# Single-transfer attention operands and new planner figures in a hybrid RWKV/attention layer

## The chip, the cores and the metric

The kernel runs on one core of a Trainium2 chip. The metric is device time in microseconds (us) of one execution; lower is better. Before the change the median of three runs is 1868.69 us (1868.56 to 1870.11).

## The reference

One decoder layer over 2048 positions of width 1024, all in float32. The input is normalised and modulated, and one projection makes the inputs of two groups of eight heads: an RWKV-7 recurrence, and a causal attention ("FoX") whose logits carry a running sum of log forget gates. Both results are gated, projected once more and normalised. Cut to what the change touches:

```python
proj = h @ w_in
q_f, k_f, v_f = (proj[..., a:b].reshape(B, T, 8, 64) for a, b in ...)
log_f = log_sigmoid(proj[..., FX_F0:FX_END] + fox_bf)
cum = cumsum(log_f, axis=1)
s = einsum('bhqd,bhkd->bhqk', q, k) * 64 ** -0.5 + cum[t] - cum[s]     # causal
y_b = softmax(s) @ v
```

## The kernel before, in words

The sequence is worked in two halves of 1024 positions, each in blocks of 512 columns. Each half has an RWKV stage and then an attention stage; the projection of w_in (66 weight tiles of 128 columns, each 48 matmuls over the two blocks of a half, 24 for a block) runs beside both and fills TensorE where the stages leave it free. A weight tile comes through a single staging buffer, `wst`, and is split by ScalarE and GpSimd into one of two buffers `wsp` (`weights`, the second generator after `plan`). All transfers are issued by SyncE, one after another, in the order in which the program was written out.

That order is made by a planner. The work is written as Python generators, and `Driver` (from line 117 on) runs them by a model of the engines: `Driver.cost` gives the duration of an instruction, `Driver.on_pe` that of a matmul by its place in the array, `Driver.time` when operands and buffers are free. The stream that can go on earliest is advanced next, and what it issues stands next on its engine's queue. The model's figures are used for nothing else, but every engine's order follows from them. For a transfer the model adds bytes over 300 GB/s and 2000 ns to the landing.

An attention logit is one fp32 product made of rounded parts. `ev_fox` stores a rounded part ("hi") and the rest ("lo") of q and k to DRAM (`qscr`, `kscr`; one tile for two heads, 128 rows of 1024 columns for hi and as many for lo; 16 evacuations of each). `ev_f` computes the running sum, its parts go to `cscr` as 3 rows per head. `qscr1` holds three rows for the q side (0, 1, 1).

In `fox_ops` each half asks for the operands of head after head: `q1` and `k1` have 67 rows (64 rows of hi and the three extra rows), `q2` and `k2` 128 rows (hi and lo). The tile pool has 21 such operands at a time. `conv` loads one operand with two transfers: 64 + 3 rows for `q1`, `k1`, and 64 + 64 rows for `q2`, `k2`. In `fox_guard` a first pass multiplies `q1` by `k1` to get the row maxima and writes their negative into one row of `q1` by a small transfer from `mrow`; `fox_s` then computes the logits from all four operands, `fox_pv` multiplies the exponentials by v. All instructions are recorded at line 134, the planner's `call`, so rows are read by tile names: `fx_s` are the attention operands, `fx_p` the exponentials, `ht` and `wsp` the projection's operands, `rw_s` the RWKV stage's, `ps` is PSUM, `arena` the general pool.

Of the kernel before, what the change touches and what calls it, by code (L numbers as in the profile page):

```python
# [9 lines left out]
F32 = mybir.dt.float32  # L10
# [8 lines left out]
TB = 1024  # L19
NB = 512  # L20
# [117 lines left out]
class Driver:  # L138
# [31 lines left out]
    def cost(self, e, op, ops, kw):  # L170
        out, ins = ops[0], ops[1:]
        n = max(a.free_size() for a in ops)
        sb = all(a.space != "PSUM" for a in ops)
        if "dma_start" in op:
            return 450.0 if e.name == "sp" else 1000.0
        if e.name == "act":
            return (94 if sb else 51) + 0.834 * n + 93 * sum(isinstance(kw.get(k), bass.AP) for k in ("scale", "bias"))
        if e.name == "dve":
            if op == "reciprocal":
                return 65 + 6.25 * n  # L180
            if op == "tensor_tensor_scan":
                return 69 + 2.15 * n
            if op == "tensor_tensor_reduce":
                return 180 + 1.04 * n
            ptr = 61 * sum(a.free_size() == 1 for a in ins[1:]) if "scalar" in op else 0
            if op in ("tensor_copy", "tensor_scalar", "memset") and sb:
                return 69 + 0.52 * n + ptr
            return 69 + 1.04 * n + ptr
        if op == "affine_select":
            return 137 + 0.834 * n  # L190
        if kw.get("op") == OP.pow:
            return 300 + 165 * n
        return 147 + 2.17 * n if op == "tensor_tensor" else 161 + 0.834 * n if op == "tensor_scalar" else 34 + 0.834 * n
# [17 lines left out]
    def on_pe(self, t, op, ops):  # L211

        m, n, k = ops[1].free_size(), ops[2].free_size(), list(ops[1].ap)[0][1]
        r0, c0 = ops[1].start_partition() // 32, ops[0].start_partition() // 32
        nr, nc = (1 if x <= 32 else 2 if x <= 64 else 4 for x in (k, m))
        one = ops[1].dtype == F32R or op == "transpose"
        stream, load = n * (1 if one else 2) / 2.4, m * 2 / 2.4
        if nr == nc == 4:
            d = max(stream + (14 if n >= 256 else 3), load + 2)
        else:  # L220
            d = max(stream + (load if nc < 4 else 6), 25.0)
        d *= 1 if one else 2
        t = max(t, self.pe.began + 7)
        if (nr, nc) != self.mode:
            t = max(t, max(max(x) for x in self.cells) + (100 if self.mode else 0))
            self.mode = (nr, nc)
        cells = [(i, j) for i in range(r0, min(4, r0 + nr)) for j in range(c0, min(4, c0 + nc))]
        t = max(t, max(self.cells[i][j] for i, j in cells))
        for i, j in cells:
            self.cells[i][j] = t + d  # L230
        self.pe.began = t + (0 if one else 7)
        self.pe.free = max(self.pe.free, t + d)
        return t + d
# [101 lines left out]
def hymba_kernel(ctx: ExitStack, tc, x, c, emb_ln_g, emb_ln_b, w_ada, b_ada, w_in, rwkv_mix, w0,  # L335
                 w_up, a0, a_up, k_k, k_a, r_k, gn_g, gn_b, fox_bf, w_out, ln_g, ln_b, out):
    nc = tc.nc
    drv = Driver()
    pe, act, dve, pool, sp = (Engine(drv, n, e) for n, e in (("pe", nc.tensor), ("act", nc.scalar),
                              ("dve", nc.vector), ("pool", nc.gpsimd), ("sp", nc.sync)))  # L340
# [3 lines left out]
    dram = ctx.enter_context(tc.tile_pool(name="dram", bufs=1, space=bass.MemoryType.DRAM))  # L344

    def dap(t, offset, ap):
        return bass.AP(tensor=t.tensor, offset=t.offset + offset, ap=ap)
# [34 lines left out]

    yscr = [dram.tile([D, TB], F32, name=f"yscr{i}") for i in range(2)]
    cscr = [dram.tile([3, 8, TB], F32, name=f"cscr{i}") for i in range(2)]
    fscr = [{k: [dram.tile([2, 128, TB] if k in "qk" else [128, TB], F32, name=f"{k}scr{h}{i}") for i in range(4)]
             for k in "qkvg"} for h in range(2)]
    qscr1 = dram.tile([3, 512], F32, name="qscr1")
    lowscr = [dram.tile([2, 128, 512], F32, name=f"lowscr{i}") for i in range(2)]
    lscr = dram.tile([128, 3, 512], F32, name="lscr")
    vscr = [[dram.tile([128, 512], F32, name=f"vscr{i}{h}") for h in range(2)] for i in range(4)]  # L390
# [185 lines left out]
    def start_consts():  # L576
# [52 lines left out]
        for i, pattern in enumerate(([[0, 32], [1, 4]], [[1, 2], [0, 64]], [[0, 2], [1, 64]])):  # L629
# [1 line left out]
            yield  # L631
            dve.tensor_copy(fb[:, i, :], jf)
            yield
        qr = yield from slots.get()
        pool.memset(qr.ap[0:3], 1.0)
        pool.memset(qr.ap[0:1], 0.0)
        sp.dma_start(qscr1, qr.ap[0:3])
# [180 lines left out]
    res = {}  # L818
# [147 lines left out]
    def ev_f(b, half, blk):  # L966

        z = yield from slots.get()
        z_ = z.ap[0:8]
        act.activation(z_, b.ap[0:8], AF.Identity, bias=bfc[0:8, 0:1])  # L970
        yield
        for i in range(1, 4):
            tt(z_, b.ap[32 * i:32 * i + 8], z_, OP.add)
            yield
        b.free()
        while nproj.get((half, blk), 0) < EF:
            yield 0
        e = yield from slots.get()
        u = yield from slots.get()
        w = yield from slots.get()  # L980
        e_, u_, w_ = e.ap[0:8], u.ap[0:8], w.ap[0:8]
        act.activation(e_, z_, AF.Abs)
        yield
        act.activation(e_, e_, AF.Exp, scale=-1.0)
        ts(z_, z_, 0.0, -8.0, OP.min, OP.mult)
        yield
        act.activation(u_, e_, AF.Ln, bias=1.0)
        ts(w_, e_, 1.0, None, OP.add)
        yield
        dve.scalar_tensor_tensor(z_, u_, 8.0, z_, op0=OP.mult, op1=OP.add)  # L990
        ts(w_, w_, -1.0, None, OP.add)
        yield
        act.activation(u_, u_, AF.Exp, scale=-1.0)
        tt(w_, e_, w_, OP.subtract)
        yield
        tt(w_, w_, u_, OP.mult)
        yield
        dve.scalar_tensor_tensor(z_, w_, 8.0, z_, op0=OP.mult, op1=OP.add)
        dve.memset(e_, 1.0)
        w.free()  # L1000
        while blk and ("f", half) not in flag:
            yield 0
        yield
        dve.tensor_tensor_scan(u_, e_, z_, bfc[0:8, 1:2], op0=OP.mult, op1=OP.add)
        yield
        dve.tensor_copy(bfc[0:8, 1:2], u_[:, 511:512])
        flag.add(("f", half))
        act.activation(z_.bitcast(F32R), u_, AF.Copy)
        yield
        tt(u_.bitcast(F32R), u_, z_, OP.subtract)  # L1010
        yield
        for i, t in enumerate((e_, z_, u_)):
            sp.dma_start(cscr[half][i, :, blk * NB:(blk + 1) * NB], t)
        for t in (z, e, u):
            t.free()

    def silu(b, g):

# [18 lines left out]
    def ev_fox(k):  # L1037
        def ev(b, half, p, blk):
            s = yield from slots.get(1)
            to = fscr[half][k][p]  # L1040
            cols = slice(blk * NB, (blk + 1) * NB)
            if k == "g":
                yield from silu(b, s)
            elif k == "v":
                act.activation(s.ap, b.ap, AF.Copy)
                b.free()
                yield
            else:
                l = yield from slots.get(1)
                act.activation(s.r, b.ap, AF.Copy)  # L1050
                yield
                tt(l.r, b.ap, s.ap, OP.subtract)
                b.free()
                i = int(k == "q")
                sp.dma_start(to[i, :, cols], s.ap)
                yield
                sp.dma_start(to[1 - i, :, cols], l.ap)
                l.free()
            if k in "vg":
                sp.dma_start(to[:, cols], s.ap)  # L1060
            s.free()
            yield
            res[half, p, k + "f", blk] = True
        return ev
# [575 lines left out]
    def fox_ops(half, st):  # L1640


        def conv(key, o, H, name, b4):
            while (b4 // 2, H // 2, name[0] + "f", b4 % 2) not in res:
                yield 0
            src = fscr[b4 // 2][name[0]][H // 2]
            c = (b4 % 2) * NB
            if name[1] == "2":
                for i in range(2):
                    sp.dma_start(o.f[hs(i)], src[i, hs(H % 2), c:c + NB])  # L1650
            else:
                sp.dma_start(o.f[0:64], src[int(name == "q1"), hs(H % 2), c:c + NB])
                sp.dma_start(o.f[64:67], cscr[b4 // 2][:, H, c:c + NB] if name == "k1" else qscr1)
            yield
            st["ops"][key] = o

        for H in range(8):
            for m in "12":
                for name, b0, b1 in (("q" + m, 2 * half, 2 * half + 2), ("k" + m, 0, 2 * half + 2)):
                    for b4 in range(b0, b1):  # L1660
                        o = yield from phase["slots"].get()
                        drv.spawn(conv((H, name, b4), o, H, name, b4), 1)
# [3 lines left out]
    def fox_guard(half, st):  # L1666
# [15 lines left out]
        def finish(H, qg, mx, left):  # L1682
# [17 lines left out]
            b.free()  # L1700
            mx.free()
            yield
            sp.dma_start(ops[H, "q1", qg].f[64:65].rearrange("o (j x) -> o j x", j=4), mrow[0:4, r].bitcast(F32))
            yield
            rowbuf.append(r)
            st["max"].add((H, qg))
# [398 lines left out]
```

## Time and profile before

| | before |
|---|---|
| median of 3 runs | 1868.69 us |
| the profiled execution's own time | 1866.47 us |
| its span, first to last instruction | 1864.7 us |
| mean granted TensorE clock | 0.98 of 2.4 GHz |
| transfers' packets | 172129, 181.60 MB |
| SyncE's queue: share of the 16 DMA engines' span | 30.6% |

The page gives each engine's busy time; a busy TensorE counts matmuls whose ends are modelled, so it isn't TensorE at its peak. Windows give the same for stretches of the span, with the granted clock (1.00 is 2.4 GHz, 0.50 is 1.2 GHz), the mean busy share of the 16 DMA engines and what they moved. The timeline names each instruction with start and duration, and in brackets the idle time before it and what ended that. The attention stages lie at about 600 to 880 us and 1300 to 1660 us, the RWKV stages before them; the tail after 1660 us is the output projection.

### The profile page before, as it was taken

The page shows a single profiled execution, that of the slowest core. Times are in us where ns is not written, and L with a number is a line of the kernel's source. Part 1 is how long each engine was busy: PE and PEld are TensorE (multiplying, and loading weights), DVE is VectorE, ACT ScalarE, POOL GpSimd, SP SyncE. Part 2 cuts the span into 40 slices and gives each one's busy share as a digit, 9 for nine tenths or more (in the row PEclk, how much of TensorE's full clock was granted, in tenths as well). Part 3 has the DMA queues.
Part 4 walks back from the last instruction along what each step waited for, and adds up shares of the span by engine and source line. Part 5 has one row for each costly group of instructions (what it writes and reads, how often), then busy time and mean ns, then how long its engine had stood idle before and what let it go on. Part 6 is the DMA issues. An engine that isn't in the chain of part 4 may idle for free.

```text
span 1864.7 us, 35565 instructions
## 1 busy us (share of the span) xinstructions
PE 1784.5 (96%) x13609; PEld 1288.3 (69%) x13609; DVE 1287.4 (69%) x3049; ACT 804.4 (43%) x1571; POOL 779.3 (42%) x773
## 2 busy tenths in 40 slices
PE   8999999999999899999999999989899899999995
PEld 6777777767777656677777777767555356666884
DVE  4987685665773768667657675762677584876998
ACT  2454555354444245554554554443244344432000
POOL 1333242422423357743143442424256364566652
PEclk8999999998999999999999999999899899999998
DMA  8252020210122755132021120213422732512433
GB/s 263 72 163 81 30 69 23 80 51 26 53 87 86 226 172 178 58 115 84 19 78 36 41 79 30 75 39 114 131 92 84 244 111 77 191 57 90 153 115 122
DMA packets 172129, 181.60 MB, mean 97 GB/s; under 512 B 12180, under 2 KB 116197, under 8 KB 171960
## 3 DMA queue, kind: packets, MB, share of 16 engines
q1 hardware_dynamic: 171960, 179.33, 30.6%
q8 instruction: 108, 1.77, 0.4%
q14 instruction: 61, 0.50, 0.1%
HBM read 132.10 MB, written 47.13 MB: 96 GB/s over the span
## 4 chain that ended last, share of the span: by engine, by line
PE 55%; DVE 5%; ACT 3%; SPq 3%; DMA 2%; issue 2%; POOL 1%; DVEq 0%; ACTq 0%; POOLq 0%
PE ps L134 55%; SPq L134 3%; ACT rw_s L134 2%; DVE rw_s L134 2%; DMA arena<-vscr 1%; DVE end_s L134 1%; DVE small L134 1%; DVE arena L134 1%; POOL rw_s L134 0%; POOL wsp L134 0%; DMA arena<-in_b_ada_dram 0%; ACT arena L134 0%; DMA yscr<-rw_s 0%; DVE fx_p L134 0%; DMA fx_s<-qscr 0%
## 5 line engine op out<-in xcount | busy, mean ns | idle before, releaser
L134 PE MATMUL ps<-ht,wsp 128*128 128x512 f32 x3840 | 976.4, 400 | 3.4 <-POOL wsp L134 1.3
L134 PEld LDWEIGHTS ps<-ht,wsp 128*128 128x128 f32 x3840 | 701.1, 189 | 163.3 <-issue 15.0
L134 POOL TENSOR_TENSOR wsp<-wst,wsp 128x1024 fp32r<-128x1024 f32 x79 | 192.8, 2440 | 320.2 <-ACT wsp L134 256.2
L134 ACT ACTIVATE rw_s<-ps 64x256 f32<-64x256 f32 (+3 forms) x544 | 215.9, 409 | 200.7 <-PE ps L134 101.0
L134 PE MATMUL ps<-fx_s 67*128 67x512 f32 (+6 forms) x960 | 261.1, 390 | 12.3 <-DMA fx_s<-kscr 4.0
L134 ACT ACTIVATE fx_p<-ps 128x512 f32<-128x512 f32 (+3 forms) x336 | 162.8, 521 | 196.2 <-PE ps L134 175.6
L134 PEld LDWEIGHTS ps<-fx_s 67*128 67x128 f32 (+1 forms) x960 | 165.4, 193 | 118.3 <-issue 47.7
L134 POOL TENSOR_TENSOR fx_p<-fx_p 128x512 f32<-128x512 f32 (+2 forms) x160 | 185.7, 1167 | 140.7 <-PE ps L134 138.3
L134 PE MATMUL ps<-rw_s 32*32 32x32 f32 (+4 forms) x5376 | 227.7, 217 | 17.0 <-DVE rw_s L134 8.0
L134 PEld LDWEIGHTS ps<-rw_s 32*32 32x32 f32 (+3 forms) x5376 | 195.7, 130 | 66.1 <-issue 26.6
L134 DVE TENSOR_TENSOR rw_s<-rw_s 128x24 f32<-128x24 f32 (+11 forms) x544 | 179.8, 336 | 26.0 <-ACT rw_s L134 12.6
L134 DVE TENSOR_REDUCE small<-ps 128x1 f32<-128x512 f32 (+1 forms) x208 | 134.5, 683 | 44.4 <-PE ps L134 43.6
L134 ACT ACTIVATE arena<-ps 128x512 f32<-128x512 f32 (+3 forms) x128 | 74.1, 581 | 191.6 <-PE ps L134 161.7
L134 POOL TENSOR_TENSOR small<-small,nhalf 128x8 f32<-128x8 f32 (+1 forms) x48 | 68.3, 1425 | 211.6 <-DVE small L134 211.5
L134 PE MATMUL ps<-fx_p,fx_v 128*64 128x512 f32 (+3 forms) x640 | 155.9, 556 | 0.0
L134 DVE TENSOR_TENSOR fx_p<-fx_p 128x512 f32<-128x512 f32 (+1 forms) x128 | 111.9, 874 | 51.6 <-POOL fx_p L134 48.9
L134 ACT ACTIVATE wsp<-wst 128x1024 fp32r<-128x1024 f32 x80 | 84.3, 1054 | 134.2 <-PE ps L134 110.1
L134 DVE TENSOR_SCALAR state<-ps,dl 64x64 f32<-64x64 f32 x256 | 72.4, 283 | 64.2 <-PE ps L134 57.2
L134 POOL TENSOR_TENSOR rw_s<-rw_s,arena 128x512 f32<-128x512 f32 x64 | 84.9, 1328 | 69.4 <-ACT arena L134 39.2
L134 DVE TENSOR_TENSOR arena<-ps,arena 128x512 fp32r<-128x512 f32 (+4 forms) x108 | 72.5, 677 | 54.0 <-ACT arena L134 50.3
L134 POOL TENSOR_SCALAR rw_s<-rw_s 64x128 f32<-64x128 f32 x128 | 38.0, 297 | 120.0 <-PE ps L134 109.4
L134 ACT ACTIVATE rw_s<-rw_s 32x256 f32<-32x256 f32 (+2 forms) x112 | 70.0, 653 | 39.4 <-DVE rw_s L134 38.7
(152 smaller groups left out, 1864.9 us busy)
## 6 DMA issues: line engine op xcount, KB each, us to landing
wst<-in_w_in_dram SPq DMA_DIRECT2D x66, 512.0 KB
fx_s<-kscr SPq DMA_DIRECT2D x144, 128.0 KB
fx_s<-qscr SPq DMA_DIRECT2D x96, 128.0 KB
ada_t<-in_w_ada_dram SPq DMA_DIRECT2D x16, 512.0 KB
rw_l<-lowscr SPq DMA_DIRECT2D x32, 256.0 KB
kscr<-arena SPq DMA_DIRECT2D x32, 256.0 KB
qscr<-arena SPq DMA_DIRECT2D x32, 256.0 KB
arena<-in_x_dram SPq DMA_DIRECT2D x16, 512.0 KB
```

Source lines behind the costliest of these rows:

```text
L134: return fn(*args, **kw)
```

## The change

What it does, in its parts:

- The DRAM tiles of q and k get a block of rows per head: `q` has 195 rows for each of two heads (three rows for 0, 1, 1; 64 of hi; 64 of lo; 64 of hi again), `k` has 131 (three of the running sum, 64 of hi, 64 of lo).
- `ev_fox` stores the 128 rows of a pair of heads into the two heads' blocks (the DRAM side of a store is 2 x 64 rows); q's hi is stored twice.
- `ev_f` copies the three rows of every head from `cscr` into `kscr`, DRAM to DRAM, four copies for each block, and those of `qscr1` into `qscr`, four for each half.
- `conv` loads an operand with one transfer: 67 rows for `q1` and `k1`, 128 rows for `q2` and `k2`. It also waits until `ev_f`'s copies have been issued.
- The row that takes the negative maximum is now row 0 of `q1` instead of row 64.
- The planner takes 600 ns instead of 450 for an issue on SyncE whose destination's first dimension is over 8, and for a matmul that doesn't fill the array `max(stream + 6, load + 5, 52)` instead of `stream + load` (or `stream + 6`, at least 25).

```diff
         if "dma_start" in op:
-            return 450.0 if e.name == "sp" else 1000.0
+            return (450.0 if list(out.ap)[0][1] <= 8 else 600.0) if e.name == "sp" else 1000.0
...
         else:
-            d = max(stream + (load if nc < 4 else 6), 25.0)
+            d = max(stream + 6, load + 5, 52.0)
...
-    fscr = [{k: [dram.tile([2, 128, TB] if k in "qk" else [128, TB], F32, name=f"{k}scr{h}{i}") for i in range(4)]
-             for k in "qkvg"} for h in range(2)]
-    qscr1 = dram.tile([3, 512], F32, name="qscr1")
+    rowsof = dict(q=[2, 195, TB], k=[2, 131, TB], v=[128, TB], g=[128, TB])
+    fscr = [{k: [dram.tile(rowsof[k], F32, name=f"{k}scr{h}{i}") for i in range(4)] for k in "qkvg"} for h in range(2)]
+    qscr1 = dram.tile([3, TB], F32, name="qscr1")
...
-        qr = yield from slots.get()
+        qr = yield from slots.get(2)
...
+        yield
+        for p in range(4):
+            sp.dma_start(dap(fscr[half]["k"][p], blk * NB, [[131 * TB, 2], [TB, 3], [1, NB]]),
+                         dap(cscr[half], 2 * p * TB + blk * NB, [[TB, 2], [8 * TB, 3], [1, NB]]))
+            if blk == 0:
+                sp.dma_start(dap(fscr[half]["q"][p], 0, [[195 * TB, 2], [TB, 3], [1, TB]]),
+                             dap(qscr1, 0, [[0, 2], [TB, 3], [1, TB]]))
+            yield
+        res[half, "cum", blk] = True
...
-                i = int(k == "q")
-                sp.dma_start(to[i, :, cols], s.ap)
+                part = lambda r: dap(to, r * TB + blk * NB, [[rowsof[k][1] * TB, 2], [TB, 64], [1, NB]])
+                sp.dma_start(part(3), s.ap)
                 yield
-                sp.dma_start(to[1 - i, :, cols], l.ap)
+                sp.dma_start(part(67), l.ap)
                 l.free()
+                if k == "q":
+                    sp.dma_start(part(131), s.ap)
...
+            while (b4 // 2, "cum", b4 % 2) not in res:
+                yield 0
             src = fscr[b4 // 2][name[0]][H // 2]
-            c = (b4 % 2) * NB
-            if name[1] == "2":
-                for i in range(2):
-                    sp.dma_start(o.f[hs(i)], src[i, hs(H % 2), c:c + NB])
-            else:
-                sp.dma_start(o.f[0:64], src[int(name == "q1"), hs(H % 2), c:c + NB])
-                sp.dma_start(o.f[64:67], cscr[b4 // 2][:, H, c:c + NB] if name == "k1" else qscr1)
+            r0, n = dict(k1=(0, 67), k2=(3, 128), q1=(0, 67), q2=(67, 128))[name]
+            sp.dma_start(o.f[0:n], src[H % 2, r0:r0 + n, (b4 % 2) * NB:(b4 % 2 + 1) * NB])
...
-            sp.dma_start(ops[H, "q1", qg].f[64:65].rearrange("o (j x) -> o j x", j=4), mrow[0:4, r].bitcast(F32))
+            sp.dma_start(ops[H, "q1", qg].f[0:1].rearrange("o (j x) -> o j x", j=4), mrow[0:4, r].bitcast(F32))
```

## Rows read from the trace of the kernel before

**Rows 1.** The page: busy time of each engine, and the chain's shares by engine

```profile
PE 1784.5 (96%) x13609; PEld 1288.3 (69%) x13609; DVE 1287.4 (69%) x3049; ACT 804.4 (43%) x1571; POOL 779.3 (42%) x773
...
PE 55%; DVE 5%; ACT 3%; SPq 3%; DMA 2%; issue 2%; POOL 1%; DVEq 0%; ACTq 0%; POOLq 0%
```

**Rows 2.** Windows by stage: us, busy PE PEld DVE ACT POOL, PEclk, DMA share, GB/s

```profile
100.00:140.00 40.00, 40.00 (x184) 31.92 (x183) 31.81 (x50) 24.02 (x37) 14.40 (x8) 1.00 0.57 179
...
600.00:880.00 280.00, 271.24 (x1462) 185.87 (x1461) 199.06 (x441) 136.43 (x264) 144.10 (x166) 0.99 0.45 140
880.00:1290.00 410.00, 397.78 (x4372) 307.04 (x4371) 263.00 (x783) 206.41 (x427) 142.83 (x151) 1.00 0.18 52
1300.00:1660.00 360.00, 344.34 (x1546) 200.63 (x1545) 249.71 (x454) 144.10 (x286) 178.76 (x179) 0.97 0.40 129
```

**Rows 3.** Windows of 10 us: the starts of both attention stages

```profile
610.00:620.00 10.00, 7.16 (x28) 5.42 (x27) 5.07 (x19) 0.82 (x2) 0.00 (x0) 0.83 0.58 166
...
630.00:640.00 10.00, 8.10 (x40) 6.29 (x38) 7.27 (x21) 3.27 (x8) 2.39 (x1) 1.00 0.97 342
...
1320.00:1330.00 10.00, 5.62 (x26) 4.32 (x24) 4.24 (x10) 0.00 (x0) 0.00 (x0) 1.00 0.71 198
1330.00:1340.00 10.00, 8.32 (x22) 5.12 (x23) 4.27 (x10) 4.26 (x8) 3.22 (x2) 0.50 0.45 139
```

**Rows 4.** Timeline of SyncE's issues from 598 to 640 us

```profile
600.76 2.02 SPq L134 DMA_DIRECT2D fx_s<-qscr  x4
...
607.22 2.51 SPq L134 DMA_DIRECT2D fx_s<-kscr  x4
...
625.53 0.41 SPq L134 DMA_DIRECT2D wst<-in_w_in_dram  x1
```

**Rows 5.** Timeline of TensorE: the first attention matmul, and the next head's

```profile
605.70 0.64 PE L134 MATMUL ps<-fx_s 67*128 67x128 f32 x3
...
615.29 0.30 PE L134 MATMUL ps<-fx_s 67*128 67x128 f32 x1 [2.84 <-DMA fx_s<-kscr]
```

**Rows 6.** Transfers by tile, 595 to 880 us: count, min/median/max ns, starts

```profile
L134 SPq DMA_DIRECT2D fx_s<-qscr x64: 444/462/1381, 600.8 to 737.7; - x64
L134 SPq DMA_DIRECT2D fx_s<-cscr x16: 415/454/456, 603.3 to 734.2; - x16
...
L134 SPq DMA_DIRECT2D kscr<-arena x8: 319/395/702, 597.6 to 814.8; - x8
L134 SPq DMA_DIRECT2D qscr<-arena x8: 320/356/572, 630.5 to 871.3; - x8
```

**Rows 7.** Transfers by tile, 1300 to 1660 us

```profile
L134 SPq DMA_DIRECT2D fx_s<-cscr x32: 238/454/465, 1303.1 to 1569.9; - x32
...
L134 SPq DMA_DIRECT2D kscr<-arena x4: 392/482/539, 1335.0 to 1455.9; - x4
L134 SPq DMA_DIRECT2D qscr<-arena x4: 319/322/342, 1525.9 to 1585.0; - x4
```

**Rows 8.** Transfers by tile, 100 to 200 us

```profile
L134 SPq DMA_DIRECT2D kscr<-arena x4: 319/352/1109, 121.6 to 129.3; - x4
...
L134 SPq DMA_DIRECT2D qscr<-arena x4: 320/366/532, 125.5 to 137.0; - x4
```

**Rows 9.** Transfers issued: destination<-source, count, KB each

```profile
fx_s<-kscr SPq DMA_DIRECT2D x144, 128.0 KB
...
kscr<-arena SPq DMA_DIRECT2D x32, 256.0 KB
```

**Rows 10.** SyncE's longest wait: us in total, times, longest

```profile
SPq L134 <- POOL wsp L134: 478.0, 59, 34.4
```

**Rows 11.** A window of 10 us in which TensorE runs projection matmuls alone

```profile
480.00:490.00 10.00, 10.00 (x48) 8.29 (x47) 6.25 (x11) 4.51 (x8) 4.73 (x5) 1.00 0.28 79
```

**Rows 12.** Timeline of TensorE: products with v, and the matmul after them

```profile
1435.72 1.98 PE L134 MATMUL ps<-fx_p,fx_v 128*64 128x512 f32 x8
...
1437.62 0.27 PE L134 MATMUL ps<-ident,small 128*4 128x128 f32 x1
```

## The prediction, made before the changed kernel was run

> **What bounds the kernel now.** I read the page first: TensorE is busy 1784.5 of the span's 1864.7 us and holds 55% of the chain that ended last [rows 1]. So no more than some 80 us of idle TensorE can be won, and whatever starves TensorE costs nearly its full length. The windows by stage say the same of the attention stages: 271 of 280 us and 344 of 360 us busy, with the sixteen DMA engines at 0.45 and 0.40 of their time, against 0.18 in an RWKV stage [rows 2]. The chain has 3% on SyncE's queue [rows 1]; the timeline shows where. At the start of an attention stage SyncE issues operand loads back to back, four 64-row loads in 2.51 us, and the next weight tile is issued only at 625.53 us, some 25 us after the first operand at 600.76 [rows 4]. TensorE gets its first attention matmul at 605.70 and idles 2.84 us before the next head's [rows 5]. The small windows show what these starts lose: 2.8 and 1.9 us in the first stage; 4.4 and 1.7 us in the second, and there 10 us at the granted clock 0.50, which is 1.2 GHz, after the engine had idled [rows 3].
>
> **What the change saves.** Fewer issues: at each start 21 operands need 42 issues at about 0.6 us (2.51 / 4 [rows 4]), afterwards 21, so SyncE is free about 12.6 us earlier. What that can give back is the idle time above: 2.8 + 1.9 + 4.4 + 1.7 = 10.8 us, plus at most about 4 us of the 8.3 busy us at half clock. I take 12 us; the ends are 0 and 15 us. Beyond the starts, fewer issues win nothing: SyncE waits 478 us for GpSimd's weight splits alone [rows 10].
>
> **What it adds on SyncE.** Sixteen third stores of q and 24 copies between DRAM tiles are 40 issues at 0.35 to 0.6 us [rows 6, 8], about 20 us spread over the span and covered by those waits; uncovered they would cost their 20 us. The first copy of each of four blocks must wait for its source to land. Behind it on SyncE stand weight loads, whose reader would come late; I take 0, with four waits of a few us, 10 us, as the other end. The new wait in `conv` is for work done long before a stage opens: 0. Setting up the longer `qscr1` and moving the maxima's row cost nothing on any path that I see.
>
> **The order.** The new matmul figures touch products on part of the array. Eight records of products with v (two fp32 passes each, two column halves side by side) hold TensorE from 1435.72 to 1437.62, 1.90 us [rows 12]. The old formula gives 0.96 us for a pair, 1.92 plus a change of array mode at 0.1 us, 2.02; the new one 0.865, 1.83 with it. So the new figure is about as near. I see no mechanism here that favours the new order: 0, ends plus and minus 9 us (0.5%).
>
> **What the change does to the transfers' shape.** This term decides. While the DMA engines are 0.97 busy they move 342 GB/s [rows 3], that is 342 / 16 / 0.97 = 22.0 GB/s each. A 64-row load is 128 KB [rows 9], so a row is 2 KB. In sixteen equal shares 64 rows are 4 rows on each engine, 0.37 us, and 128 rows 8 on each, 0.74 us. The new loads of `q1` and `k1` have 67 rows, a prime, which sixteen engines can't share equally. The two ends: an uneven split with at most 5 rows on one engine, 0.47 us; or one engine for all 67, 137 KB / 22.0 GB/s = 6.2 us. The new stores have 2 x 64 rows on the DRAM side: either 8 rows on each engine as now, or, shared by the leading 2, 64 rows on each of two engines, 6.0 us. No row shows a transfer of such a shape. I take the upper ends: the large transfers listed have 64 or 128 rows, which every power of two up to 16 divides, so nothing in the trace shows that an uneven share exists at all, and the only equal share of a prime is one engine.
>
> [...]
>
> **The sum, if so.** Take the busiest engine.
> - First attention stage, 600 to 880: 16 `k1` (one for each three-row load) and 16 `q1` (64 loads from `qscr` for 16 `q1`, their 16 three-row loads and 32 halves of `q2`) [rows 6] are 32 x 6.2 = 198 us. `q2` and `k2`: 32 x 0.74 = 24. The 8 + 8 stores become 8 + 12 at 6.0: 120. The rest: 0.45 x 280 = 126 us of DMA time [rows 2] less 48 for what was just counted at its old price, 78. Together 420 us in a stage of 280. Ten of the stores are late in it, up to 871.3, and drain in the RWKV stage behind it, where the engines are 0.18 busy: 60 us less. That leaves 360, plus 80 us.
> - Second, 1300 to 1660: 32 `k1` [rows 7] and 16 `q1` are 298 us, `q2` and `k2` 36, 4 + 6 stores 60, the rest 0.40 x 360 = 144 [rows 2] less 59, 85. Together 479 in 360. I take plus 100 of the 119, since what lands last is needed only by the last head.
> - The first stores, 121 to 137 us: 4 + 6 at 6.0 are 60 us of one engine [rows 8], while TensorE is 40.00 of 40 us busy on projections [rows 2] and a weight tile lasts it 10 us (48 matmuls in 10 us [rows 11]). Two tiles are held ahead, 20 us; plus 30 us after one more is half hidden.
> - The other groups of stores meet RWKV stages: 0, the other end 30; I take 20.
>
> What turns this into TensorE's time: the backlog stands in front of the weight tiles too, so the projection can't fill the holes; SyncE, which waits for each weight tile to be used, then issues later operands late as well. Sum: 80 + 100 + 30 + 20 - 12 = 218 us over the profiled execution's 1866.5, that is 2084; the median of the runs shown stands 2.2 us higher, 2087. I put the forecast at **2090 us**. Upper end: nothing drains elsewhere, 140 + 119 + 60 + 30 us, and each of some fifteen weight tiles in the two stages leaves the engine idle for the split (a few us, 60 in all): 409, or 2280. Lower end: half of the sum, 1980.
>
> **The rivals.**
> 1. One engine, but hidden by prefetch (slower still): operands are asked for up to 21 ahead, and only the first three loads of each stage show, 3 x 6.2 = 18.6 us against about 5 now. Twice 13.6 us over 1868.7: 1896. Against it: 420 us of work for one engine in 280 us of stage can't be hidden by any depth. For it: where each head's loads are used over 35 us (280 / 8), four of them take 25.
> 2. No slowdown but a gain: transfers of any shape are spread over the engines. Then only the 12 us and the order count: 1868.7 - 12 = 1857. For it speaks that the starts are bound by SyncE's issues [rows 4, 5]; it decides if a 67-row load takes no more than about 0.5 us of its busiest engine.
> 3. A wash: spread evenly, and the gain at the starts goes to other waits there, such as the load at 0.97 DMA share [rows 3], which fewer issues don't shorten: 1869.
>
> **How the numbers follow.** About 0.2%, 3.7 us, can be told from no change. I give the forecast 0.68, rival 1 0.12, rival 2 0.14, rival 3 0.06. Hence slower 0.80, same 0.06, faster 0.14. The range 1860 to 2280 holds the forecast's own (1980 to 2280) but for some 0.07, rivals 1 and 3, and the upper part of rival 2; it leaves out about 0.17.
>
> **What would show it.** Right: windows in which TensorE idles for tens of us in both attention stages while the mean DMA share is low, since one engine in sixteen works; waits of ScalarE for weight tiles and of TensorE for `fx_s<-kscr` and `fx_s<-qscr` among the longest; the first attention matmul some 15 us later after the stage opens; granted clock 0.50 there. The page should show 160 operand loads for 320. Wrong: a mean DMA share at the starts as high as now, the first attention matmul earlier, and the idle 2.8 and 4.4 us gone. Then the shares are even, and the time lies below 1869.

## The result, and the profile after

The changed kernel takes 2298.72 us (median of four runs, 2291.08 to 2305.52), against 1868.62 us: a ratio of 1.2298, 95% interval 1.2255 to 1.2341. It is 430 us slower. Slower was forecast, with the right cause; the time lies 19 us above the range, and the loss is twice the 218 us of the sum.

The page of the changed kernel: busy time by engine, the SyncE queue's transfers, and the chain.

```profile
PE 1887.4 (82%) x13609; PEld 1333.6 (58%) x13609; DVE 1278.5 (55%) x3049; ACT 804.9 (35%) x1571; POOL 772.7 (34%) x773
...
q1 hardware_dynamic: 170584, 183.91, 25.0%
...
PE 18%; DMA 7%; SPq 4%; DVE 2%; issue 0%; POOL 0%; ACT 0%; ACTq 0%; POOLq 0%
```

TensorE issues the same 13609 matmuls as in [rows 1]. Its idle time went from 80 to 416 us (2303.8 less 1887.4), and its busy time grew by 103 us although the work is the same. Together they are the difference of the two spans: 336 + 103 = 439 us. The next view says where. Its windows (us, busy PE PEld DVE ACT POOL, PEclk, DMA share, GB/s) are: the first stores; the first attention stage, now 671 to 1010; the second RWKV stage; the second attention stage; and two pieces of 50 us at the starts of the attention stages.

```profile
120.00:200.00 80.00, 63.72 (x521) 48.33 (x520) 40.91 (x97) 29.24 (x52) 25.07 (x18) 0.89 0.35 108
671.00:1010.00 339.00, 210.37 (x994) 132.11 (x995) 127.43 (x291) 92.06 (x194) 106.49 (x143) 0.74 0.25 83
1010.00:1594.00 584.00, 539.88 (x5017) 414.21 (x5015) 334.70 (x913) 258.23 (x507) 185.66 (x179) 0.96 0.23 72
1594.00:2180.00 586.00, 424.14 (x1693) 233.64 (x1694) 313.12 (x565) 154.72 (x304) 223.15 (x215) 0.82 0.24 80
...
700.00:750.00 50.00, 14.78 (x63) 11.82 (x63) 9.35 (x27) 3.95 (x7) 1.76 (x2) 0.64 0.17 60
1600.00:1650.00 50.00, 14.76 (x38) 9.08 (x36) 16.55 (x38) 1.44 (x4) 0.00 (x0) 0.55 0.16 55
```

Read the last two rows first. TensorE works 15 of 50 us, and the DMA engines, which should be the cause, are only 0.17 and 0.16 busy, which is fewer than three of sixteen on the mean. A starved TensorE beside a low mean share is what the prediction had named as the sign of one engine at work: in [rows 3] the share was 0.97 at such a place. The granted clock is 0.64 and 0.55 on the mean in these two windows and 0.885 over the run, where it was 0.980 before, and the 103 us of longer busy time fit that: the same work at a lower clock. In this trace one projection matmul starts 427 ns after another at the median where the clock is 0.50, and 227 ns where it is 1.00; 512 columns in 427 ns are 1.2 a ns.

What the transfers became, in the list of issues (count, KB each):

```profile
fx_s<-kscr SPq DMA_DIRECT2D x48, 256.0 KB
...
fx_s<-kscr SPq DMA_DIRECT2D x48, 134.0 KB
fx_s<-qscr SPq DMA_DIRECT2D x32, 134.0 KB
...
kscr<-cscr SPq DMA_DIRECT2D x16, 12.0 KB
```

There are 160 operand loads, as the change says; the 48 + 32 of 134 KB are the 67-row ones. SyncE's timeline at the start of the second attention stage shows what one of them costs (start, duration of the issues together, count):

```profile
1595.07 0.72 SPq L134 DMA_DIRECT2D fx_s<-qscr  x2
1595.83 21.32 SPq L134 DMA_DIRECT2D fx_s<-kscr  x4
1617.19 6.17 SPq L134 DMA_DIRECT2D fx_s<-qscr  x2
1623.40 2.52 SPq L134 DMA_DIRECT2D fx_s<-kscr  x4
1625.97 5.86 SPq L134 DMA_DIRECT2D fx_s<-qscr  x2
1631.88 21.43 SPq L134 DMA_DIRECT2D fx_s<-kscr  x4
```

Two `q1` are issued in 0.72 us; the four `k1` behind them take 21.32 us, the next head's 21.43 us: 5.3 us each on the mean, where an issue took 0.6 us in [rows 4]. The two 128-row loads behind them take 6.17 us, the next four 2.52 us. The semaphore updates in the trace say when these transfers landed: the 67-row loads one after another, 5.1 to 5.7 us apart, and the first of the 128-row loads, issued at 1617.19, only at 1631.61, after the last of them. So SyncE issued no faster here than these loads were worked off, and 137 KB in 5.3 us are 26 GB/s, near the 22.0 GB/s of one engine that the prediction took from [rows 3], not sixteen times that. The window from 1636 to 1653 us, in which 67-row loads alone are under way, shows 26 GB/s at a mean DMA share of 0.07: about one engine of sixteen.

TensorE's timeline in the first attention stage, with the idle time in brackets; these answer to [rows 5]:

```profile
693.47 1.08 PE L134 MATMUL ps<-fx_s 67*128 67x128 f32 x3 [12.51 <-DMA fx_s<-kscr]
...
717.59 0.77 PE L134 MATMUL ps<-fx_s 67*128 67x128 f32 x2 [11.54 <-DMA fx_s<-kscr]
```

The first attention matmul comes 21.9 us after the first operand's issue at 671.62, against 4.9 us before. And waits (us in total, times, longest): TensorE's longest, and ScalarE's for what comes through `wst`, which is weight tiles and, for the output projection, the gated results from `yscr`:

```profile
PE ps L134 <- DMA fx_s<-kscr: 179.6, 17, 15.5
...
ACT wsp L134 <- DMA wst<-yscr: 58.9, 3, 40.8
...
ACT wsp L134 <- DMA wst<-in_w_in_dram: 49.3, 8, 17.0
```

The projection could not fill the holes. To see it, the stages must be cut alike, from the first operand's issue to the last product with the exponentials. In the kernel before these are 600.8 to 799.9 us and 1300.5 to 1720.2 us, 199 and 420 us long, and not the 280 and 360 us of the section on the time before: its first window takes in 80 us that are nearly all projection, and its second ends 60 us early. The two windows of the kernel before, and its projection matmuls in them (count, busy us, mean ns of one, idle time before them):

```profile
600.80:799.90 199.10, 190.34 (x1044) 121.69 (x1043) 137.74 (x312) 92.58 (x197) 113.89 (x144) 0.99 0.49 154
1300.50:1720.20 419.70, 404.04 (x1833) 239.94 (x1832) 290.82 (x513) 161.35 (x319) 219.30 (x211) 0.97 0.38 122
...
L134 PE MATMUL ps<-ht,wsp 128*128 128x512 f32 x252 | 69.2, 403 | 0.1
...
L134 PE MATMUL ps<-ht,wsp 128*128 128x512 f32 x461 | 122.9, 399 | 1.1 <-ACT fx_p L134 0.8 <-DVE ht L134 0.3
```

and of the changed kernel, 671.6 to 1008.7 and 1595.1 to 2189.1 us:

```profile
671.60:1008.70 337.10, 209.07 (x988) 131.07 (x989) 126.75 (x290) 91.64 (x193) 105.19 (x143) 0.74 0.25 83
1595.10:2189.10 594.00, 433.11 (x1747) 240.63 (x1746) 318.42 (x580) 155.00 (x305) 225.09 (x217) 0.82 0.24 79
...
L134 PE MATMUL ps<-ht,wsp 128*128 128x512 f32 x196 | 66.1, 464 | 0.0
...
L134 PE MATMUL ps<-ht,wsp 128*128 128x512 f32 x391 | 110.4, 413 | 3.8 <-POOL wsp L134 2.6 <-ACT fx_p L134 0.8 <-ACT mrow L134 0.4
```

The first stage is 138 us longer and yet holds 56 projection matmuls fewer, the second 174 us longer with 70 fewer. At 0.21 us each ([rows 11]: 48 in 10 us) these are 12 and 15 us of work that other stages must do, so the two attention stages lost 150 and 189 us, of 439 in all. In the first stage a projection matmul takes 337 ns of busy time (66.1 / 196) where it took 275 (69.2 / 252), at a mean granted clock of 0.74 instead of 0.99.

### The profile page after: what moved, and what is told of

Same layout as the page of the kernel before. It is cut to its first block, busy times and chain, and to the rows that moved or that the text cites. A ratio compares the mean times of both kernels' runs of the same rounds, so it can differ in the third digit from the quotient of the medians.

```text
span 2303.8 us, 35419 instructions
## 1 busy us (share of the span) xinstructions
PE 1887.4 (82%) x13609; PEld 1333.6 (58%) x13609; DVE 1278.5 (55%) x3049; ACT 804.9 (35%) x1571; POOL 772.7 (34%) x773
## 5 line engine op out<-in xcount | busy, mean ns | idle before, releaser
L134 PE MATMUL ps<-ht,wsp 128*128 128x512 f32 x3840 | 1009.9, 410 | 20.0 <-ACT wsp L134 7.5
L134 PEld LDWEIGHTS ps<-ht,wsp 128*128 128x128 f32 x3840 | 717.9, 194 | 199.1 <-issue 29.1
L134 PE MATMUL ps<-fx_s 67*128 67x512 f32 (+5 forms) x960 | 292.0, 426 | 216.2 <-DMA fx_s<-kscr 179.6
L134 PEld LDWEIGHTS ps<-fx_s 67*128 67x128 f32 (+1 forms) x960 | 182.3, 213 | 349.0 <-issue 243.0
L134 PE MATMUL ps<-rw_s 32*32 32x32 f32 (+4 forms) x5376 | 232.5, 219 | 20.6 <-DVE rw_s L134 11.4
L134 PE MATMUL ps<-fx_p,fx_v 128*64 128x512 f32 (+3 forms) x640 | 176.5, 604 | 1.1 <-ACT ht L134 0.8
L134 DVE CUSTOM_DVE_ANT_0 ps<-ps,mneg 128x128 f32<-128x128 f32 (+3 forms) x128 | 61.7, 504 | 135.4 <-PE ps L134 134.9
L134 DVE TENSOR_TENSOR arena<-ps,arena 128x512 f32<-128x512 f32 (+4 forms) x108 | 72.8, 678 | 106.4 <-ACT arena L134 67.7
L134 DVE TENSOR_SCALAR state<-ps,dl 64x64 f32<-64x64 f32 x256 | 72.4, 283 | 63.7 <-PE ps L134 58.6
L134 ACT ACTIVATE arena<-ps,pc 128x512 f32<-128x512 f32 x70 | 49.3, 709 | 127.1 <-PE ps L134 66.0
```

Source lines behind the costliest of these rows:

```text
L134: return fn(*args, **kw)
```

## The experiments

Three theories stood against each other. **Shares:** as the prediction had assumed, a transfer runs on as many engines as can share its leading rows equally, so 67 rows run on one, and 2 x 64 rows on two. **Order:** the planner's new figures make an order that starves TensorE. **Copies:** the new copies between DRAM tiles and the waits for their sources hold SyncE.

**e1: loads of 80 rows.** The 13 extra rows are the next ones in the block and are not read.

```diff
-            r0, n = dict(k1=(0, 67), k2=(3, 128), q1=(0, 67), q2=(67, 128))[name]
+            r0, n = dict(k1=(0, 80), k2=(3, 128), q1=(0, 80), q2=(67, 128))[name]
```

> The changed kernel with one number altered: q1 and k1 are loaded with 80 rows instead of 67 (13 rows of the low part come along and are not read), which 16 engines can share equally at 5 rows each. More bytes, nothing else. Shares theory (a 67-row load runs on one DMA engine, a store to 2 x 64 rows on two): the 80 loads drop from about 6 us to about 0.5 us of their busiest engine, the 80 stores still hold two engines for about 6 us each, so about 2000 us (1930 to 2120), and the waits of TensorE for fx_s<-kscr fall from 180 us to under 20. Order theory (the planner's new figures make an order that starves TensorE): 2300 us as before this edit, within 2%. Copies theory (the DRAM to DRAM copies and the waits for their sources hold SyncE): 2300 us too.

Measured: 1992.4 us, ratio 1.0683 (1.0659 to 1.0706). Moving a fifth more bytes in each of these loads takes 306 us off, and TensorE's waits for `fx_s<-kscr` fall from 179.6 to 2.7 us. The copies are those of the changed kernel, so the copies theory can't hold for this part. The order isn't quite the same: the planner reckons with a transfer's bytes, and in the two traces 2362 of TensorE's 13609 matmuls stand at another place. For the order theory e6 is the cleaner test.

**e2: stores of 64 rows, loads left at 67.**

```diff
-                part = lambda r: dap(to, r * TB + blk * NB, [[rowsof[k][1] * TB, 2], [TB, 64], [1, NB]])
-                sp.dma_start(part(3), s.ap)
+                def store(r, a):
+                    for h in range(2):
+                        sp.dma_start(dap(to, (h * rowsof[k][1] + r) * TB + blk * NB, [[TB, 64], [1, NB]]), a[hs(h)])
+                store(3, s.ap)
...
```

(and `store` in the same way for the rows from 67 and 131 on)

> The changed kernel with the stores of q and k cut into two transfers of 64 rows, one for each head; loads stay at 67 rows. Shares theory: the stores go to all 16 engines at 4 rows each, the 80 loads of 67 rows still hold one engine for about 6 us each, most of them in the attention stages: about 2150 us (2050 to 2240), with the gain in the projection and RWKV stages. Order theory and copies theory: 2300 us within 2%.

Measured: 2167.86 us, 1.1618 (1.1593 to 1.1643). Twice as many stores take 131 us off.

**e3: both.**

> Both edits: loads of 80 rows and stores of 64 rows. Shares theory: nothing is left of the slowdown, and the few us of fewer issues at the stage starts show: 1845 to 1885 us, TensorE's granted clock back at 0.98. Order theory: still far above 2200 us. Copies theory: above 1950 us, since the copies and their waits are still there.

Measured: 1864.01 us, 0.9992 (0.9973 to 1.0011): the whole loss is gone, with the copies, the new layout and the new figures still in. The two parts add: the stores alone are worth 1992.4 - 1864.0 = 128 us, the loads alone 2167.9 - 1864.0 = 304 us, together 432 of the 435 us between the changed kernel and e3. For the stores this is no matter of order: e1 and e3 differ in the place of 6 of TensorE's 13609 matmuls. SyncE's timeline of e3 at the same place of the first attention stage:

```profile
607.17 0.85 SPq L134 DMA_DIRECT2D fx_s<-qscr  x2
608.08 1.23 SPq L134 DMA_DIRECT2D fx_s<-kscr  x2
609.35 1.18 SPq L134 DMA_DIRECT2D fx_s<-qscr  x2
```

The issues take 0.4 to 0.6 us each again. TensorE's waits for these operands fall to

```profile
PE ps L134 <- DMA fx_s<-kscr: 3.3, 3, 1.6
```

The stores show the same. Issues into `qscr` and `kscr` from the pool (count, min/median/max ns) in the changed kernel, and into `qscr` in e3:

```profile
L134 SPq DMA_DIRECT2D qscr<-arena x49: 269/3224/6424, 66.0 to 1573.6; - x49
...
L134 SPq DMA_DIRECT2D kscr<-arena x32: 478/524/5109, 122.5 to 1544.7; - x32
```

```profile
L134 SPq DMA_DIRECT2D qscr<-arena x97: 269/587/684, 66.7 to 1324.2; - x97
```

A store of q to 2 x 64 rows holds SyncE for 3.2 us at the median, one of k for 0.5 us and at most 5.1; two of 64 rows take 0.6 us each.

What the 67-row loads cost by stage, e2 and e3 show, whose stores are the same. The attention stages of e2, then those of e3, cut as above; they hold the same number of projection matmuls but for one (240 and 406, against 239 and 406):

```profile
605.00:923.60 318.60, 204.67 (x1032) 131.26 (x1031) 133.56 (x303) 93.11 (x197) 108.94 (x144) 0.81 0.28 91
1454.50:2049.30 594.80, 432.40 (x1762) 242.46 (x1762) 317.10 (x579) 156.84 (x307) 227.94 (x218) 0.83 0.24 80
...
607.20:800.70 193.50, 188.06 (x1031) 119.32 (x1031) 129.09 (x304) 92.29 (x197) 110.18 (x144) 0.99 0.52 154
1330.90:1750.80 419.90, 406.73 (x1762) 233.51 (x1761) 334.52 (x580) 155.31 (x307) 237.28 (x218) 0.96 0.36 116
```

That is 125 us in the first stage and 175 us in the second, 300 of the 304 us. The slow stores cost elsewhere. In e1, which keeps them, the first operand is issued at 669.8 us, 63 us later than in e3 (607.17 above), with 27 projection matmuls more done (6 us); its attention stages are nearly as long as e3's (206.8 and 419 us).

**e4: the planner's figures alone,** in the kernel before.

```diff
-            return 450.0 if e.name == "sp" else 1000.0
+            return (450.0 if list(out.ap)[0][1] <= 8 else 600.0) if e.name == "sp" else 1000.0
...
-            d = max(stream + (load if nc < 4 else 6), 25.0)
+            d = max(stream + 6, load + 5, 52.0)
```

> The kernel before with the planner's new figures alone (600 ns for an issue over 8 rows, the new matmul formula); all transfers as before. Shares theory: 1869 us within 15 us either way. Order theory: most of the 430 us, over 2150 us.

Measured: 1877.73 us, 1.007 (1.0049 to 1.009). The order theory falls as an explanation of the loss; the figures cost 11 us here.

**e6: loads of 68 rows** (stores of 64), a dose between 67 and 80.

```diff
-            r0, n = dict(k1=(0, 67), k2=(3, 128), q1=(0, 67), q2=(67, 128))[name]
+            r0, n = dict(k1=(0, 68), k2=(3, 128), q1=(0, 68), q2=(67, 128))[name]
```

> Like e3, with loads of 68 rows. By equal shares 68 rows go to 4 engines, 17 rows each, about 1.5 us instead of 0.45 (80 rows) or 6 (67 rows). If cost comes from the backlog of an engine that is asked for more than it can do in a stage, 1.5 us stay far below that (48 x 1.5 = 72 us in a stage of 360) and the time is e3's 1864 us or up to 20 us more. If each transfer costs in proportion to its busiest engine's time (304 us for 5.6 us against 0.4), it is 1864 + 64 = 1928 us. If 67 is special for another reason than its shares (an odd or an unaligned row count), 68 behaves like 80.

Measured: 1936.16 us, 1.0361 (1.0312 to 1.0409). Against e2 this settles the order and the copies. By tile names and shapes, e2 and e6 hold the same matmuls, transfers and other instructions in the same order on every engine; their loads differ by one row, 67 and 68, and that row takes 232 us off. Neither a different order nor a copy can have made this part.

Over e3 it is 72 us, close to the 64 us of the proportional reading and far from the other two. The order of e3 differs from e6's (1819 of 13609 matmuls stand elsewhere), and further down orders alone move the time by 7 to 22 us, so 72 us is a reading with some of that in it. It still decides against the way in which the prediction had summed: 48 loads of 1.6 us (an estimate: 17 rows on each of four engines, at the 22.0 GB/s from [rows 3]) can't overfill any engine in an attention stage, and yet they cost time. What costs isn't only what exceeds the stage.

The traces show how the shapes differ. In the changed kernel, from 147 to 149 us, stores to 2 x 64 rows and one of the copies are all that is under way, and the mean DMA share is 0.13, about two engines of sixteen, at 51 GB/s; for the 67-row loads above it is 0.07. In e3, from 600 to 640 us, with stores of 64 rows and loads of 80 and 128 rows among the transfers, it is 1.00. In e6 the 68-row loads land 1.2 to 1.8 us apart in the first attention stage, where the 67-row loads above land 5.1 to 5.7 us apart: 139 KB in 1.5 us are 93 GB/s, by the 22.0 GB/s of [rows 3] the rate of about four engines, which is an estimate. All this is as the shares theory has it. The number of updates that a transfer makes to its semaphore differs as well: counted in the trace of the changed kernel, 16 for each load of 128 rows, 3 for each of the 80 stores to 2 x 64 rows and 2 for each of the 80 loads of 67 rows. How such a number comes about no run shows.

**e9: e6 with a planner that knows.** Transfers as in e6; the model lets each such load hold one queue, holds SyncE once that queue is over 12 us behind, and lands nothing before it is empty.

```diff
-            end = self.dma + (2000.0 if e.name == "sp" else 2800.0)
+            al = list(out.ap)
+            if al[0][1] in (67, 68) or (al[0][1] == 2 and al[1][1] == 64):
+                self.one = max(self.one, e.free) + 1430.0
+                e.free = max(e.free, self.one - 12000.0)
+            end = max(self.dma, self.one) + (2000.0 if e.name == "sp" else 2800.0)
```

> e6 with a planner that knows what a load of 68 rows does: each holds one queue for 1430 ns, and nothing lands before that queue is empty. The transfers are e6's. If the 72 us of e6 over e3 are work that stands, in the order written out, behind an operand that lands later than planned, a planner that knows puts other work there and most of them come back: 1865 to 1895 us. If they are the transfers' own length, whatever the order: 1936 us within 10 us.

Measured: 1896.55 us, 1.0175 (1.0154 to 1.0196), just above the first of the expected brackets: 40 of the 72 us come back with the same transfers. TensorE's wait for operands, in e6 and in e9:

```profile
PE ps L134 <- DMA fx_s<-kscr: 30.1, 13, 4.8
```

```profile
PE ps L134 <- DMA fx_s<-kscr: 15.5, 8, 3.8
```

**e10: the changed kernel with such a planner** (5600 ns in place of 1430).

> The changed kernel with a planner that knows its transfers: 5600 ns of one queue for each load of 67 rows and each store to 2 x 64 rows, SyncE held once that queue is over 12 us behind, and nothing landing before it is empty. If order decides here too: under 2200 us. If the busiest engine's own work and SyncE's held issues bound the stages whatever the order (80 x 5.6 + 80 x 5.4 = 880 us of one engine): 2250 to 2330 us.

Measured: 2135.3 us, 1.1445 (1.1416 to 1.1475). This order gives back 163 of 435 us; 271 stay. Whether a better order would give back more was not tried.

**e13: e2 with that planner,** for the loads alone.

> e2 (loads of 67 rows, stores of 64) with the planner of e10, which knows that a 67-row load holds one queue for 5600 ns. e2 stood 304 us over e3. In e10 the knowledge gave back 163 us of the whole. If that was the loads' share, late operands in a fixed order: 2168 less 130 to 170, 2000 to 2040 us, and TensorE's waits for fx_s<-kscr drop below 100 us from 178. If it came from the stores: 2150 to 2180 us.

Measured: 2031.73 us, 1.0882 (1.0857 to 1.0907). Of the loads' 304 us, 136 come back with the same transfers in another order, as they would if work had stood behind late operands; 168 stay. TensorE's waits for the operands, in e2 and in e13:

```profile
PE ps L134 <- DMA fx_s<-kscr: 178.0, 17, 16.1
```

```profile
PE ps L134 <- DMA fx_s<-kscr: 74.9, 17, 15.6
```

**e7: two transfers for each operand,** otherwise e3 with its loads of 67 rows cut into 3 + 64, and those of 128 into 64 + 64.

```diff
-            sp.dma_start(o.f[0:n], src[H % 2, r0:r0 + n, (b4 % 2) * NB:(b4 % 2 + 1) * NB])
+            cut = (0, 3, 67) if n == 67 else (0, 64, 128)
+            for a, z in zip(cut, cut[1:]):
+                sp.dma_start(o.f[a:z], src[H % 2, r0 + a:r0 + z, (b4 % 2) * NB:(b4 % 2 + 1) * NB])
```

> Like e3 (new layout, new figures, stores of 64 rows), but each operand again by two transfers (3 + 64 rows, 64 + 64 rows) as in the kernel before. If fewer issues at the stage starts are worth the 12 us that the prediction put on them: 1876 us (1870 to 1884), near e4's 1878. If they are worth nothing: 1864 us within 4 us, and TensorE's idle time at the starts of the attention stages is the same in both.

Measured: 1884.35 us, 1.0091 (1.0072 to 1.0111). Single transfers are worth 20 us against it, where 12 were forecast. The two orders differ as well, and the next runs show that orders alone move the time by such amounts, so 20 us is a reading with the order in it.

**The figures, taken apart.** e5 is e3 with both old figures, e8 the changed kernel with both old figures, e11 and e12 the kernel before with one new figure each, e14 is e5 with the new matmul figure.

> Loads of 80 rows, stores of 64 rows, and the planner's figures of the kernel before. If the new figures cost here what they cost alone in e4 (11 us), this is 1853 us (1846 to 1859), a gain of 0.7% over the kernel before, which is what single transfers give. If the figures fit the new transfers and cost nothing there, it is 1864 us, like e3, within 4 us.

> The changed kernel with the planner's figures of the kernel before, transfers as changed. If the figures' 11 us add to the rest: 2288 us (2270 to 2300). If the new figures spread the stalled issues better or worse, it lies elsewhere by more than 1%: a planner that takes 450 for 600 ns packs transfers closer.

> The kernel before with the new matmul figure alone. e4 (both figures) stood 11 us over the kernel before. If the matmul figure makes that: 1874 to 1882 us; if it is nearer to the chip and helps: 1855 to 1864 us.

> The kernel before with the new issue figure alone (600 ns over 8 rows). If it makes e4's 11 us: 1874 to 1882 us; if the matmul figure makes them: 1864 to 1870 us.

> e5 (80-row loads, 64-row stores) with the new matmul figure and the old issue figure. e5 is 0.4% under the kernel before, and the matmul figure alone (e11) is 0.4% under it. If the two add: 0.992, 1852 us. If orders differ by some us for no reason that adds up, anything from 1853 to 1872 us.

| | matmul figure | issue figure | us | ratio (interval) |
|---|---|---|---|---|
| e11, transfers as before | new | old | 1859.39 | 0.9961 (0.9947 to 0.9976) |
| e12, as before | old | new | 1867.76 | 1.0011 (0.9996 to 1.0026) |
| e4, as before | new | new | 1877.73 | 1.007 (1.0049 to 1.009) |
| e5, 80 and 64 rows | old | old | 1859.67 | 0.9962 (0.9945 to 0.998) |
| e14, 80 and 64 rows | new | old | 1842.33 | 0.987 (0.9848 to 0.9892) |
| e3, 80 and 64 rows | new | new | 1864.01 | 0.9992 (0.9973 to 1.0011) |
| e8, as changed | old | old | 2357.01 | 1.2634 (1.2599 to 1.2669) |

The matmul figure gains 6.5 us alone and 17 us on the mended transfers. The issue figure does nothing alone, but beside the matmul figure it costs 18 and 22 us. In the changed kernel the pair saves 58 us; why was not tried. The single figures' effects don't add, so no rule about them follows; e5 lies between its two expectations, and e14 below both of its own. e14 is also 1.3% below the kernel before and 20% below the changed one. Its page:

```profile
PE 1777.8 (97%) x13609; PEld 1279.7 (70%) x13609; DVE 1299.1 (71%) x3049; ACT 798.2 (43%) x1569; POOL 784.0 (43%) x773
...
PE 87%; DMA 4%; ACT 3%; DVE 3%; POOL 1%; issue 1%; SPq 1%; ACTq 0%; DVEq 0%; POOLq 0%
```

TensorE idles 58.5 us (1836.3 us of span less 1777.8) instead of 80, and SyncE's queue holds 1% of the chain instead of 3%.

## Why the prediction was wrong

**What bounds the kernel, and starving TensorE:** right. The loss is TensorE's idle time (336 us) and its longer busy time (103 us), which goes with the lower granted clock (0.885 against 0.980).

**The shape of the transfers:** right. The upper end was taken for both, the author's choice, which no row of the kernel before had shown, and e1, e2 and e6 confirm it: with 80 rows no loss is left, 68 cost 72 us, 67 cost 304 us, 2 x 64 rows cost 128 us. The price of a 67-row load was put at 6.2 us; issues and landings show 5.3. A smaller price makes the sum smaller, so the price isn't what failed. The share of the DMA engines agrees: 0.07 with 67-row loads alone under way and 0.13 with the stores, about one and two of the sixteen.

**The step that failed is the sum:** "Together 420 us in a stage of 280 ... 60 us less. That leaves 360, plus 80 us", and so for each stage. It counted only what the busiest engine has to do beyond the stage's length, and let the rest run beside TensorE. For the loads alone this way of counting gives 198 + 24 + 78 = 300 us in 280 and 298 + 36 + 85 = 419 in 360, 20 and 59 us over; e2 and e3 measured 125 and 175. The stages' lengths had been misread, too. With 199 and 420 us, and the rest in proportion, it would be some 78 and 13 us over, 91 in all against 300. And e6, which by this counting costs nothing, costs 72 us.

What each load adds to the time is a share of its own length. At the prediction's price, 80 loads of 6.2 us instead of 0.47 are 458 us of one engine, and 304 us or 66% of it came back in the time; for 68 rows (by the estimate under e6 17 rows on each of four engines, 35 KB at 22.0 GB/s, 1.6 us) it is 72 of 90 us. The stores had a smaller share: 80 of 6.0 us instead of 0.74 are 421 us of two engines, and 128 us came back, 30%.

Three things stood in the way of the overlap. The order is fixed, and work stands behind operands that the planner believed to have landed (136 of the 304 us come back in another order, e13). SyncE is held by the issue itself (5.3 us on the mean at the start of the second attention stage), so weight tiles and everything else on its queue come late too, which the text had only from waits for weight tiles; what this costs by itself no run shows. And TensorE worked at a lower granted clock, 0.74 and 0.82 in the two attention stages where it had been 0.99 and 0.97: its busy time grew by 103 us, for which the sum had no term at all. Cut by stage as above, the first attention stage lost 150 us where 80 were put down, and the second 189 us where 100 were.

**The first stores:** plus 30 us was the right kind. 120 to 200 us shows TensorE busy for 63.7 of 80 us, 16 us lost in this place alone; up to the first operand's issue e1 shows 57 us (63 less 6), and all stores together cost 128 us. From the end of the first attention stage to the second's first operand e1 takes 587.7 us against e3's 530.2, with 13 projection matmuls more, some 55 us lost there. So the stores cost little in the attention stages, where the sum charged them, and much in the RWKV stages, where it let ten of them drain free and put the other groups at 20 us.

**The saving of fewer issues:** 12 us was forecast; e7 against e3 gives 20, e5 against the kernel before, with the old figures in both, 6.7 us. Both readings hold an order of their own; as far as they tell, the term was of the right size.

**The order:** 0 with ends of plus and minus 9 us. The figures alone cost 11 us (e4), 2 us outside, and between orders 17 to 22 us lie in the mended kernel. In the changed kernel itself the new figures saved 58 us (e8); without them the loss would have been larger still. The ends were too close.

**Added issues on SyncE, and `conv`'s new wait:** put at 0. e3 and e14 contain them all, and 80 more stores, and stand level with or below the kernel before.

**Rival 1** (one engine, hidden by prefetch, 1896 us) is refuted by the time and by the wait of 179.6 us for operands, **rivals 2 and 3** by e1. What they describe is what e3 and e5 are.

## What to carry to other kernels

Before merging transfers, look at the shape that both sides get. Here loads of 67 rows alone kept 0.07 of the sixteen engines busy, and stores to 2 x 64 rows 0.13, while with transfers of 64, 80 and 128 rows the share came to 1.00 in e3; loads of 68 rows landed 1.2 to 1.8 us apart, those of 67 rows 5.1 to 5.7, and padding 67 rows to 80 took 306 us off. When TensorE starves while the mean DMA share is low (here 0.16 and 0.17), suspect transfers that run on few engines, and look for issues on SyncE that last microseconds. In a kernel with a written-out order, count a late load as a share of its own length (here two thirds to four fifths), not as what exceeds a stage, and tell the planner what its transfers really take. Read the bounds of a stage from its first and last instruction before reckoning with its length.

## What the hardware showed that was not expected

Issues on SyncE lasted about as long as the transfers ahead of them took to be worked off: 5.3 us on the mean for the 67-row loads after the first two, which land 5.1 to 5.7 us apart, 3.2 us at the median for a store of q to 2 x 64 rows, against 0.4 to 0.6 us in e3. That the engine's queue is full at these times is a reading; how much it holds no run shows. A transfer of another shape behind these loads landed late too: the 128-row load issued at 1617.19 us landed at 1631.61, after the last 67-row load ahead of it. With 68 rows no such long issue of an operand shows in e6 (0.83 us at most), and the cost seems to come from late landing alone, as the waits for operands (30.1 us against e3's 3.3) suggest; the rest of e6's 72 us was not taken apart.
